# Three buffers instead of two and of four, a later mean square, and weight rounding at priority, in a two-layer hybrid trunk step

## The chip, the cores and the metric

The kernel runs on one core of a Trainium2 chip. The metric is the device time of one execution in microseconds (us). The median of three runs is quoted; one further execution was profiled.

## The reference, cut to what matters

One inference step of two layers over 1024 latent tokens and 256 context tokens, model width 1024. Each layer does:

```
h = rms_norm(x) * (1 + scale) + shift                      # scale, shift, gate from the condition
aq, ak, av, ag, bq, bk, bv, bg, cx, cg, ga, gb, gc = split(h @ w_in)
qa, ka = rope_2d(rms_norm(aq)), rope_2d(rms_norm(ak))      # latents only are rotated
ya = window_attention(qa, ka, av, cached keys, sink) * silu(ag)
qb, kb = rms_norm(bq), rms_norm(bk)                        # per head of 64, over the head's channels
yb = neighbourhood_attention(qb, kb, bv, cached keys, bias) * silu(bg)
yc = rglru(depthwise_conv(cx)) * silu(cg)
z = sigmoid(ga) * (ya @ w_br[0]) + sigmoid(gb) * (yb @ w_br[1]) + sigmoid(gc) * (yc @ w_br[2])
x = x + gate * (z @ w_out)
```

Branch A has 8 query heads and 2 key heads and rotary positions; branch B has 8 heads of each and no rotation. Context tokens read only context tokens. The outputs are the two token arrays and the new keys, values and recurrent states.

## The kernel before, in words

Activations lie with channels on the 128 partitions and tokens along the free dimension, in chunks of 512, 512 (latents) and 256 (context). To hold float32 accuracy, each operand of a projection is split in two parts, hi (rounded) and lo (the rest), and a product takes three matmuls: hi x hi, lo x hi, hi x lo. A weight tile of 128 x 512 is loaded (`load_w`, L415, ring "wr" of 2), rounded on ScalarE to hi (`split_w`, L423) and subtracted on GpSimd to lo (L424), into rings of 4. `job` is one projection of 128 output columns over its chunks: 24 matmuls for each chunk, then an `evac` that takes the result out of PSUM. The weights of the next job are asked for when a job starts.

A planner (class `Weave`) orders TensorE's instructions by hand while the program is written: it adds up an estimated time `now`, runs the attention chain when its parts are due, fills the rest with dense jobs from two queues (`need`: the projections that attention needs; `spare`: gates), and calls functions put off with `W.later(delay, fn)` when `now` reaches them. Delays stand in the table `T`, in ns; `T["ms"]` is the delay of the mean square. TensorE keeps exactly this order. The order on the other engines and on the DMA queue of SyncE is chosen by a scheduler from each instruction's priority, which is its place in the program; `tc.high_priority(AHEAD)` with `AHEAD = 400` gives instructions the priority of a place 400 earlier. Each engine then runs its list in order.

In `attention`, `qk_norm` takes a chunk of q or k out of PSUM: the square on ScalarE (L738, ring "qsq" of 3) and a scaled copy on VectorE (L739, ring "qraw"), both at high priority. `finish`, T["ms"] later, sums the squares over the channels on TensorE (`q_ms`, `k_ms`), makes the reciprocal root on ScalarE and VectorE (L745 to L756) and, in branch A for latents, loads the rotary tables (`cs`, L759, ring "stage") and rotates on GpSimd (L761 to L763). `to_dram` makes the hi and lo parts on GpSimd (L773, L774, ring "stage") and sends them to memory (L780 for k, L869 and L872 for q). For v, `evac` copies to a "qraw" tile (L834), and T["v"] later four transposes and a split on ScalarE (L428) and VectorE (L429) make the parts `vs` in the ring "stage". Cached keys (`kc`) and values (`vc`) are loaded into "qraw" tiles as well. The attention chain works through groups of 256 queries: score products `sc` and `sl` into the PSUM ring "s" of 2, row minima on VectorE (L985, L1001, and L1004 with the sink), exponentials on ScalarE (L1007, L1009), transposes of P (`pt`), their split (`PT`, L428 and L429), and the value products `o`.

Of the kernel before, what the change touches and what calls it, by code (L numbers as in the profile page):

```python
# [9 lines left out]
F32 = mybir.dt.float32  # L10
F32R = mybir.dt.float32r
# [4 lines left out]
P = 128  # L16
# [9 lines left out]
HD = 64  # L26
# [48 lines left out]
AHEAD = 400  # L75
# [1 line left out]
PSB = {"d": 2, "s": 2, "t": 3, "o": 1}  # L77
LGB = ("s", "t")
LDB = ("d", "t")
T = dict(f1=9, f2=2, kc=10000, c0=10000, cq=1, gx=3, nx=8000, yo=1500, yi=1000, aq=9000, ac=7000, ms=2000, v=3200, tok=8600, scale=1100, t0=3400, tb=2200, o=2200, soft=7600, pace=9000, lg=320, lr=8500, cv=16000, le=4200)  # L80


class Weave:
# [107 lines left out]
def trunk(nc, tc, ctx, I, K, O):  # L191
# [22 lines left out]
    def f32(ap):  # L214
        return ap.bitcast(F32)
# [160 lines left out]
    def ada_chain(chunks, ap):  # L376
# [7 lines left out]
        ws = load(quads[0])  # L384
        at = W.now + T["aq"]
        for i, (l, n, h) in enumerate(quads):
# [33 lines left out]
    def split_w(r, name, wp=wp):  # L420
        hi = wp.tile([P, 4, P], F32R, tag="wh", name=f"{name}_h", bufs=4)
        lo = wp.tile([P, 4, P], F32R, tag="wl", name=f"{name}_l", bufs=4)
        nc.scalar.copy(hi, r)  # L423
        nc.gpsimd.tensor_sub(lo, r, f32(hi))  # L424
        return [(hi[:, k], lo[:, k]) for k in range(4)]

    def split(hi, lo, x):
# [300 lines left out]
    def attention(l, H, ap):  # L728
# [2 lines left out]


        def qk_norm(ps, N, gain, rope_c0, name, then, blocks=False):
            raw = ap.tile([P, 512], F32, tag="qraw", name=f"{name}_raw", bufs=4)
            sq = ap.tile([P, 512], F32, tag="qsq", name=f"{name}_sq", bufs=3)
            src, to = (blocked(ps), in_blocks) if blocks else (ps, lambda t: t)
            with tc.high_priority(AHEAD):
                nc.scalar.activation(to(sq[:, :N]), src, AF.Square)  # L738
                nc.vector.tensor_scalar(to(raw[:, :N]), src, gain, None, ALU.mult)  # L739

            def finish():
                ms = ps_tile("t", f"{name}_ms")
                mm(ms[:, :N], blk, sq[:, :N], True, True)
                me = cp.tile([P, 512], F32, tag="g2", name=f"{name}_me", bufs=3)
                nc.vector.tensor_scalar(me[:, :N], ms[:, :N], EPS, None, ALU.add)  # L745
                if not loaded:
                    exp_ln(me[:, :N])
                    loaded.append(True)
                rs = sq

                nc.scalar.activation(rs[:, :N], me[:, :N], AF.Ln)
                nc.scalar.activation(rs[:, :N], rs[:, :N], AF.Exp, scale=-0.5)
                nc.vector.tensor_tensor(raw[:, :N], raw[:, :N], rs[:, :N], ALU.mult)
                nc.scalar.activation(rs[:, :N], rs[:, :N], AF.Square)
                nc.vector.tensor_tensor(rs[:, :N], me[:, :N], rs[:, :N], ALU.mult)
                nc.vector.scalar_tensor_tensor(raw[:, :N], rs[:, :N], -3.0, raw[:, :N], ALU.add, ALU.mult)  # L756
                if rope_c0 is not None:
                    cs = ap.tile([P, 2, 512], F32, tag="stage", name=f"{name}_cs", bufs=2)
                    dma(cs, K["k_rope"][:, :, rope_c0:rope_c0 + N])  # L759
                    nc.vector.stream_shuffle(rs, raw, [(i + 16) % 32 for i in range(32)])  # L760
                    nc.gpsimd.tensor_tensor(rs, rs, cs[:, 1], ALU.mult)  # L761
                    nc.gpsimd.tensor_tensor(raw, raw, cs[:, 0], ALU.mult)
                    nc.gpsimd.tensor_add(raw, raw, rs)  # L763
                then(raw[:, :N])
            W.later(T["ms"], finish)

        def to_dram(x, N, name, put, psum=False):
            st = ap.tile([P, 2, 512], F32R, tag="stage", name=f"{name}_st", bufs=2)
            hi, lo = st[:, 0, :N], st[:, 1, :N]
            if psum:  # L770
                split(hi, lo, x)
            else:
                nc.gpsimd.tensor_copy(hi, x)  # L773
                nc.gpsimd.tensor_sub(lo, x, f32(hi))  # L774
            for h in range(2):
                put(h, f32(st[h * HD:(h + 1) * HD, :, :N]))
# [6 lines left out]
        def k_jobs(br, p, cond):  # L783
            name = f"{br}{l}_{p}"
            perm, rope = br == 1, br == 0
            c0w = O_BK + p * P if br else O_AK
            h0 = 2 * p if br else 0
            out = O[4] if br else O[2]

            def start():  # L790
                t = ap.tile([P, 4, P], F32, tag="qraw", name=f"kc{name}", bufs=4)
                src = I["cache_kb"] if br else I["cache_ka"]
                dma(t, src[0, l, :, h0:h0 + 2].rearrange("(j p) h d -> p j (h d)", p=P))

                def cached():
                    pt = ps_tile("t", f"kct{name}")
                    for j in range(4):
                        transpose(pt[:, j * P:(j + 1) * P], t[:, j], ident)
                    to_dram(pt, NPAST, f"kc{name}", k_put(br, p, NTOK, NPAST), True)
                W.later(T["kc"], cached)  # L800

            def evac(ci, ps):
                c0, N = CHUNKS[ci]

                def then(kn):
                    if c0 >= NLAT:
                        def to_tokens():
                            pt = ps_tile("t", f"kt{name}")
                            for j in range(2):
                                transpose(pt[:, j * P:(j + 1) * P], kn[:, j * P:(j + 1) * P], ident)  # L810
                            ko = ap.tile([P, 2, P], F32, tag="Y", name=f"ko{name}", bufs=2)
                            with tc.high_priority(AHEAD):
                                nc.scalar.copy(ko, pt[:, :2 * P].rearrange("p (j m) -> p j m", j=2))  # L813
                            dma(out[0, l, :, h0:h0 + 2].rearrange("(j p) h d -> p j (h d)", p=P), ko)
                        W.later(T["tok"], to_tokens)
                    to_dram(kn, N, f"k{name}_{ci}", k_put(br, p, c0, N))
                    W.mark(("K", br, l, p, ci), 4000)
                qk_norm(ps, N, dcol[l][:, 2 * br + 1:2 * br + 2], c0 if rope and c0 < NLAT else None,
                        f"k{name}_{ci}", then, perm and c0 < NLAT)
            W.need.append((cond, job(w_in, c0w, (0, 1, 2), lambda ci: H.cols(ci), evac, f"k{name}", start)))  # L820

        def v_jobs(br, p, cond):
            name = f"{br}{l}_{p}"
# [4 lines left out]

            def evac(ci, ps):
                c0, N = CHUNKS[ci]  # L830
                vr = ap.tile([P, 512], F32, tag="qraw", name=f"vr{name}_{ci}", bufs=4)
                lat = perm and c0 < NLAT
                with tc.high_priority(AHEAD):
                    nc.scalar.copy(in_blocks(vr) if lat else vr[:, :N], blocked(ps) if lat else ps)  # L834

                def finish():
                    pt = ps_tile("t", f"vt{name}_{ci}")
                    nb = N // P
                    for j in range(nb):
                        transpose(pt[:, j * P:(j + 1) * P], vr[:, j * P:(j + 1) * P], ident)  # L840
                    src = pt[:, :N].rearrange("p (j h d) -> p j h d", j=nb, h=2)
                    st = ap.tile([P, 4, 2, 2, HD], F32R, tag="stage", name=f"vs{name}_{ci}", bufs=2)
                    split(st[:, :nb, :, 0], st[:, :nb, :, 1], src)
                    if lat:

                        for h in range(2):
                            dma(v_d[l][br][p][ci * HD:(ci + 1) * HD, h:8:2], f32(st[h * HD:(h + 1) * HD]))
                    else:
                        dma(v_d[l][br][p][:, c0 // P:c0 // P + nb], f32(st[:, :nb]))
                    if c0 >= NLAT:  # L850
                        vo = ap.tile([P, 2, P], F32, tag="Y", name=f"vo{name}", bufs=2)
                        nc.scalar.copy(vo, pt[:, :2 * P].rearrange("p (j m) -> p j m", j=2))
                        dma(out[0, l, :, h0:h0 + 2].rearrange("(j p) h d -> p j (h d)", p=P), vo)
                    W.mark(("V", br, l, p, ci), 4000)
                W.later(T["v"], finish)
# [25 lines left out]
        class Keys:  # L881
# [16 lines left out]

            def load_v(c):
                h0 = 2 * c.p if c.br else 0  # L900
                t = ap.tile([P, 4, 2, HD], F32, tag="qraw", name=f"vc{c.name}", bufs=4)
                src = I["cache_vb"] if c.br else I["cache_va"]
                dma(t, src[0, l, :, h0:h0 + 2].rearrange("(j p) h d -> p j h d", p=P))
                c.V = {}
# [653 lines left out]
```

## Time and profile before

| what | us |
|---|---|
| median of 3 runs (3121.65 to 3123.55) | 3122.75 |
| the profiled execution | 3122.02 |
| its span, from the first to the last instruction | 3120.2 |
| TensorE busy in it | 3067.6 |
| VectorE, ScalarE, GpSimd busy | 1781.0, 1707.6, 973.2 |
| mean granted clock of TensorE, of full speed | 0.995 |

Busy time counts an instruction from its start to its end; a bracket at the end of a row of the timeline is the idle time of that engine just before, and what released it. A row of a window has its bounds and length, the busy time of TensorE, of its weight loads, of VectorE, ScalarE and GpSimd with the instructions of each, the granted clock, the DMA share and GB/s. PE is TensorE, PEld its weight loads, DVE VectorE, ACT ScalarE, POOL GpSimd, SPq the queue of SyncE. A clock of 1.00 is 2.4 GHz, 0.50 is 1.2 GHz; a figure between them is a stretch that has both.

### The profile page before, as it was taken

How to read it: one execution, taken by the hardware profiler on the slowest of the kernel's cores; microseconds unless marked ns; L12 is line 12 of the kernel's file. 1: busy time of each engine (PE TensorE's matmuls, PEld its weight loads, DVE VectorE, ACT ScalarE, POOL GpSimd, SP SyncE). 2: the span in 40 equal slices, each digit the busy share in tenths (PEclk: the TensorE clock that was granted, in tenths of full speed). 3: DMA queues.
4: the chain of work that ended last, by engine and by line, in shares of the span. 5: the costliest groups of instructions: out<-in, count | busy, mean ns of one | idle time of the engine just before them, and what ended most of it. 6: DMA issues, size and time to landing. Idle time of an engine off the chain costs nothing. (4 is left out here: it accounts for less than half of the span.)

```text
span 3120.2 us, 48035 instructions
## 1 busy us (share of the span) xinstructions
PE 3067.6 (98%) x17421; PEld 2620.8 (84%) x17421; DVE 1781.0 (57%) x3293; ACT 1707.6 (55%) x3587; POOL 973.2 (31%) x811
## 2 busy tenths in 40 slices
PE   8999999999999999999999999999999999999999
PEld 5777888888888888888878888888888888888887
DVE  5666366666566564356373563665666666655541
ACT  5667365555555664444346873655655656654422
POOL 3454322222222021236243443212232221212632
PEclk9999999999999999999999999999999999999999
DMA  8554545545533332663442226455455332337543
GB/s 290 166 174 133 170 133 159 162 110 163 163 102 86 94 97 77 227 200 127 146 140 68 80 87 181 121 154 147 118 158 153 103 100 78 96 133 238 176 152 102
DMA packets 445322, 433.98 MB, mean 139 GB/s; under 512 B 75056, under 2 KB 366492, under 8 KB 443804
## 3 DMA queue, kind: packets, MB, share of 16 engines
q1 hardware_dynamic: 439100, 413.87, 44.3%
q0 software_dynamic: 5664, 16.83, 1.6%
q8 instruction: 137, 2.24, 0.3%
q14 instruction: 101, 0.83, 0.1%
q10 hardware_dynamic: 320, 0.21, 0.0%
HBM read 297.07 MB, written 137.29 MB: 139 GB/s over the span
## 5 line engine op out<-in xcount | busy, mean ns | idle before, releaser
L428 ACT CAST PT<-pt 128x512 fp32r<-128x512 f32 (+2 forms) x528 | 273.6, 536 | 302.2 <-PE pt L225 298.3
L429 DVE TENSOR_TENSOR PT<-pt,PT 128x512 fp32r<-128x512 f32 (+2 forms) x528 | 321.2, 622 | 102.3 <-ACT PT L428 99.7
L985 DVE TENSOR_REDUCE st<-sc 128x1 f32<-128x512 f32 x256 | 176.1, 688 | 258.4 <-PE sc L218 258.0
L218 PE MATMUL gt<-hhl,wgt_h 128*128 128x512 f32 x736 | 299.0, 406 | 1.3 <-ACT wgt_h L423 1.3
L218 PE MATMUL gt<-hhl,wgt_l 128*128 128x512 f32 x736 | 290.0, 394 | 1.1 <-POOL wgt_l L424 1.1
L218 PE MATMUL gt<-hll,wgt_h 128*128 128x512 f32 x736 | 290.2, 394 | 0.0
L225 PE MATMUL pt<-cst,P 128*128 128x128 f32 x1856 | 272.7, 273 | 0.7 <-ACT ko L813 0.2
L424 POOL TENSOR_TENSOR wgt_l<-wgt_r,wgt_h 128x512 fp32r<-128x512 f32 x110 | 175.2, 1602 | 304.3 <-ACT wgt_h L423 297.3
L225 PEld LDWEIGHTS pt<-cst,P 128*128 128x128 f32 x1856 | 217.6, 141 | 5.8 <-DVE k_me L745 1.4
L218 PE MATMUL po<-z,wpo_h 128*128 128x512 f32 (+1 forms) x768 | 207.5, 358 | 1.2 <-ACT wpo_h L423 1.2
L1007 ACT ACTIVATE P<-sc,st 128x512 f32<-128x512 f32 x256 | 175.1, 684 | 57.7 <-DVE st L1001 55.8
L218 PE MATMUL br<-yl,wbr_h 128*128 128x512 f32 (+1 forms) x576 | 205.2, 356 | 0.6 <-DVE yl L429 0.6
L218 PE MATMUL br<-yh,wbr_h 128*128 128x512 f32 (+1 forms) x576 | 204.7, 355 | 0.0
L218 PE MATMUL br<-yh,wbr_l 128*128 128x512 f32 (+1 forms) x576 | 204.4, 355 | 0.0
L424 POOL TENSOR_TENSOR wsg_l<-wsg_r,wsg_h 128x512 fp32r<-128x512 f32 x48 | 64.6, 1350 | 369.9 <-ACT wsg_h L423 341.6
L1009 ACT ACTIVATE P<-sl,st 128x384 f32<-128x384 f32 (+1 forms) x320 | 170.6, 533 | 13.0 <-DVE st L997 12.8
L218 PE MATMUL o<-PT,Vpast 128*128 128x256 f32 x1024 | 176.0, 293 | 0.9 <-DVE PT L429 0.3
L218 PE MATMUL sc<-Kpast,Q 128*128 128x512 f32 x512 | 168.9, 411 | 7.2 <-ACT P L1007 7.1
L218 PEld LDWEIGHTS gt<-hhl,wgt_l 128*128 128x128 f32 x736 | 138.6, 188 | 33.8 <-POOL wgt_l L424 1.5
L218 PEld LDWEIGHTS gt<-hhl,wgt_h 128*128 128x128 f32 x736 | 138.8, 189 | 32.3 <-issue 4.7
L218 PEld LDWEIGHTS gt<-hll,wgt_h 128*128 128x128 f32 x736 | 139.1, 189 | 25.7 <-issue 0.5
L218 PE MATMUL sg<-hhl,wsg_h 128*128 128x512 f32 x384 | 155.7, 405 | 0.0
(350 smaller groups left out, 8495.5 us busy)
## 6 DMA issues: line engine op xcount, KB each, us to landing
Q<-q_d SPq DMA_DIRECT2D x160, 256.0 KB
gl<-g_d SPq DMA_DIRECT2D x48, 640.0 KB
wgt_r<-in_w_in_dram SPq DMA_DIRECT2D x110, 256.0 KB
g_d<-tgt SPq DMA_DIRECT2D x92, 256.0 KB
wa<-in_w_ada_dram POOLq DMA_DIRECT2D x64, 256.0 KB, 4.1
yg<-y_d SPq DMA_DIRECT2D x24, 640.0 KB
yr<-s_d SPq DMA_DIRECT2D x24, 640.0 KB
wpo_r<-in_w_out_dram SPq DMA_DIRECT2D x60, 256.0 KB
```

The costliest lines, as they stand in the source:

```text
L218: nc.tensor.matmul(out, a, b, start=start, stop=stop)
L225: nc.tensor.transpose(out, x, idn)
L424: nc.gpsimd.tensor_sub(lo, r, f32(hi))
L428: nc.scalar.copy(hi, x)
L429: nc.vector.tensor_sub(lo, x, f32(hi))
L985: nc.vector.tensor_reduce(cm, psc, AX.X, ALU.min)
L1007: nc.scalar.activation(pt[:, nl * P:(nl + 4) * P], psc, AF.Exp, bias=m, scale=-1.0, accum_out=sums[:, t, x, 1:2])
L1009: nc.scalar.activation(pt[:, :nl * P], loc, AF.Exp, bias=m, scale=-1.0, accum_out=sums[:, t, x, 0:1])
```

## The change

The ring "stage" gets three buffers instead of two, for the parts and for the rotary tables. The ring "qraw" gets three instead of four, for raw q, k and v and for the cached keys and values. The mean square is planned 3.2 us instead of 2.0 us after the eviction. The rounding of weights and its subtraction get high priority, in every stage of the kernel. The number of instructions does not change.

```diff
-T = dict(... ms=2000, v=3200, ...)
+T = dict(... ms=3200, v=3200, ...)
...
     def split_w(r, name, wp=wp):
         hi = wp.tile([P, 4, P], F32R, tag="wh", name=f"{name}_h", bufs=4)
         lo = wp.tile([P, 4, P], F32R, tag="wl", name=f"{name}_l", bufs=4)
-        nc.scalar.copy(hi, r)
-        nc.gpsimd.tensor_sub(lo, r, f32(hi))
+        with tc.high_priority(AHEAD):
+            nc.scalar.copy(hi, r)
+            nc.gpsimd.tensor_sub(lo, r, f32(hi))
...
         def qk_norm(ps, N, gain, rope_c0, name, then, blocks=False):
-            raw = ap.tile([P, 512], F32, tag="qraw", name=f"{name}_raw", bufs=4)
+            raw = ap.tile([P, 512], F32, tag="qraw", name=f"{name}_raw", bufs=3)
...
-                    cs = ap.tile([P, 2, 512], F32, tag="stage", name=f"{name}_cs", bufs=2)
+                    cs = ap.tile([P, 2, 512], F32, tag="stage", name=f"{name}_cs", bufs=3)
...
         def to_dram(x, N, name, put, psum=False):
-            st = ap.tile([P, 2, 512], F32R, tag="stage", name=f"{name}_st", bufs=2)
+            st = ap.tile([P, 2, 512], F32R, tag="stage", name=f"{name}_st", bufs=3)
...
-                vr = ap.tile([P, 512], F32, tag="qraw", name=f"vr{name}_{ci}", bufs=4)
+                vr = ap.tile([P, 512], F32, tag="qraw", name=f"vr{name}_{ci}", bufs=3)
...
-                    st = ap.tile([P, 4, 2, 2, HD], F32R, tag="stage", name=f"vs{name}_{ci}", bufs=2)
+                    st = ap.tile([P, 4, 2, 2, HD], F32R, tag="stage", name=f"vs{name}_{ci}", bufs=3)
```

The "qraw" tiles of the cached keys and values change from 4 to 3 buffers in the same way.

## Rows read from the trace of the kernel before

**Rows 1.** The page, part 1: engine, busy us, share of span, instructions

```profile
PE 3067.6 (98%) x17421; PEld 2620.8 (84%) x17421; DVE 1781.0 (57%) x3293; ACT 1707.6 (55%) x3587; POOL 973.2 (31%) x811
```

**Rows 2.** TensorE waits, whole span: releaser, us in total, times, longest

```profile
PE sc L218 <- ACT P L1007: 7.1, 15, 0.9
PE q_ms L218 <- ACT q_sq L738: 4.9, 2, 2.5
```

**Rows 3.** Timeline, layer 0, 801 to 808 us: start, length, instruction, [wait before]

```profile
801.61 2.92 SPq L872 DMA_DIRECT2D q_d<-q_st  x4
...
805.97 0.59 ACT L428 CAST vs<-vt 128x512 fp32r<-128x512 f32 x1 [6.98 <-DMA q_d<-q_st]
...
807.09 0.39 PE L218 MATMUL o<-PT,Vlat 128*128 128x256 f32 x1 [3.86 <-ACT PT L428]
807.93 1.92 PE L218 MATMUL o<-PT,Vlat 128*128 128x256 f32 x7 [0.45 <-DVE PT L429]
```

**Rows 4.** Windows of 5 us, layer 0: busy by engine, granted clock, DMA

```profile
805.00:810.00 5.00, 2.46 (x9) 1.94 (x10) 1.71 (x3) 2.96 (x8) 0.00 (x0) 0.84 0.60 209
810.00:815.00 5.00, 5.00 (x22) 4.71 (x22) 2.76 (x5) 2.39 (x6) 0.00 (x0) 0.50 0.00 0
```

**Rows 5.** Timeline, layer 1, 2358 to 2363 us, ScalarE and TensorE

```profile
2358.20 0.59 ACT L428 CAST vs<-vt 128x512 fp32r<-128x512 f32 x1 [2.44 <-DMA q_d<-q_st]
...
2361.40 0.62 PE L218 MATMUL o<-PT,Vlat 128*128 128x256 f32 x3 [1.26 <-DVE PT L429]
2362.39 1.01 PE L218 MATMUL o<-PT,Vlat 128*128 128x128 f32 x4 [0.37 <-ACT PT L428]
```

**Rows 6.** Timeline, first q of branch A, layer 0: evictions, last read

```profile
768.13 0.61 ACT L738 ACTIVATE q_sq<-q 128x512 f32<-128x512 f32 x1
...
784.75 0.39 ACT L738 ACTIVATE q_sq<-q 128x256 f32<-128x256 f32 x1
...
786.25 1.83 POOL L774 TENSOR_TENSOR q_st<-q_raw,q_st 128x512 fp32r<-128x512 f32 x1
```

**Rows 7.** Timeline and one window, mean squares: 891 to 900 us, 2447 us

```profile
891.71 2.98 POOL L424 TENSOR_TENSOR wgt_l<-wgt_r,wgt_h 128x512 fp32r<-128x512 f32 x2
...
893.47 1.23 DVE L1004 TENSOR_TENSOR st<-st,sink 128x1 f32<-128x1 f32 x1
...
895.51 0.19 ACT L1007 ACTIVATION_READ_ACCUMULATOR P<-sc,st 128x1 f32 x1
...
896.59 0.75 PE L218 MATMUL q_ms<-q_sq,cst 128*128 128x256 f32 x2 [2.52 <-ACT q_sq L738]
...
895.00:900.00 5.00, 3.42 (x12) 3.07 (x13) 3.79 (x11) 2.05 (x7) 0.00 (x0) 0.71 0.55 161
...
2447.85 0.70 PE L218 MATMUL q_ms<-q_sq,cst 128*128 128x256 f32 x2 [2.42 <-ACT q_sq L738]
```

**Rows 8.** Timeline and one window, weights: 233 to 265 us, 1592 to 1595 us

```profile
233.14 3.03 SPq L415 DMA_DIRECT2D wgt_r<-in_w_in_dram  x2
...
258.73 1.15 ACT L423 CAST wgt_h<-wgt_r 128x512 fp32r<-128x512 f32 x2
...
259.41 0.50 PE L218 MATMUL gt<-hhl,wgt_h 128*128 128x512 f32 x1 [1.28 <-ACT wgt_h L423]
...
261.25 0.50 PE L218 MATMUL gt<-hhl,wgt_l 128*128 128x512 f32 x1 [1.10 <-POOL wgt_l L424]
...
260.00:265.00 5.00, 3.90 (x12) 2.97 (x12) 5.00 (x4) 1.04 (x1) 3.62 (x3) 0.72 0.20 59
...
1592.63 0.73 PE L218 MATMUL po<-z,wpo_h 128*128 128x512 f32 x2 [1.17 <-ACT wpo_h L423]
1594.21 0.50 PE L218 MATMUL po<-z,wpo_l 128*128 128x512 f32 x1 [0.84 <-POOL wpo_l L424]
```

**Rows 9.** ScalarE's waits, whole span: weight roundings that wait for loads

```profile
ACT wgt_h L423 <- DMA wgt_r<-in_w_in_dram: 28.1, 16, 5.1
...
ACT wk_h L423 <- DMA wk_r<-in_w_in_dram: 5.7, 5, 2.5
```

More of the change, by code (lines that the diff above doesn't have):

```diff
@@ L79 @@
 LDB = ("d", "t")
-T = dict(f1=9, f2=2, kc=10000, c0=10000, cq=1, gx=3, nx=8000, yo=1500, yi=1000, aq=9000, ac=7000, ms=2000, v=3200, tok=8600, scale=1100, t0=3400, tb=2200, o=2200, soft=7600, pace=9000, lg=320, lr=8500, cv=16000, le=4200)
+T = dict(f1=9, f2=2, kc=10000, c0=10000, cq=1, gx=3, nx=8000, yo=1500, yi=1000, aq=9000, ac=7000, ms=3200, v=3200, tok=8600, scale=1100, t0=3400, tb=2200, o=2200, soft=7600, pace=9000, lg=320, lr=8500, cv=16000, le=4200)
 class Weave:
@@ L790, in start @@
             def start():
-                t = ap.tile([P, 4, P], F32, tag="qraw", name=f"kc{name}", bufs=4)
+                t = ap.tile([P, 4, P], F32, tag="qraw", name=f"kc{name}", bufs=3)
                 src = I["cache_kb"] if br else I["cache_ka"]
@@ L900, in load_v @@
                 h0 = 2 * c.p if c.br else 0
-                t = ap.tile([P, 4, 2, HD], F32, tag="qraw", name=f"vc{c.name}", bufs=4)
+                t = ap.tile([P, 4, 2, HD], F32, tag="qraw", name=f"vc{c.name}", bufs=3)
                 src = I["cache_vb"] if c.br else I["cache_va"]
```

## The prediction

> **What bounds the kernel now.** I read the page's busy shares first. TensorE is busy 98% of the span and the other engines are far below it [rows 1], so adding or removing work on ScalarE, VectorE or GpSimd matters only where TensorE waits for it, and the change adds and removes none: it moves work and resizes rings. What it can win is TensorE's idle time, 3120.2 - 3067.6 = 52.6 us, and what the engine loses while its clock is granted at the lower of its two levels (1.2 instead of 2.4 GHz). The second view is TensorE's list of waits, then the timeline of TensorE window by window, because the sizes of single waits tell which part of the change could touch them. In the attention stages the waits are few and long, except for a row of short ones, the score product waiting for an exponential that frees its PSUM bank, 15 waits of 7.1 us in total [rows 2]. The third view is the windows of 5 us, for the clock behind each long wait.
>
> **Part 1: a third buffer for the parts ("stage", 2 to 3).** The ring holds both the hi/lo parts on their way to memory and the rotary tables. In layer 0 the parts of two q chunks fill both slots. Their four transfers are issued from 801.61 us on; the parts of v, which come next on ScalarE, wait 6.98 us for such a transfer to land [rows 3]. ScalarE runs in order, so the rounding of P transposes queued behind it comes late too, and TensorE waits 3.86 us and then 0.45 us more for those: 4.31 us [rows 3]. From there its clock is at the lower level: granted 0.84 in 805 to 810 and 0.50 in 810 to 815 us [rows 4], with TensorE busy nearly all the time after the wait. The loss is 0.16 x 5 + 0.50 x 5 = 3.3 us. With a third slot the v parts go ahead when ScalarE comes to them, at 805.97 - 6.98 = 799.0 us. Next would be the P parts: about 0.6 us of ScalarE for v, 0.6 for P and 0.7 of VectorE, done by about 802 us if nothing else comes first, ahead of the product that began at 807.09 after 3.86 us of wait, so wanted at 803.2. So both go, 4.3 + 3.3 = 7.6 us. In layer 1 the same v parts wait 2.44 us and TensorE 1.26 + 0.37 = 1.6 us [rows 5], with no loss of clock. Sum of part 1: 9.2 us. The lower bound is 1.6 us, if in layer 0 a new wait of the same kind takes the old one's place.
>
> **Part 2: the ring of raw q, k, v (4 to 3).** A slot is held from the eviction to the last read by GpSimd. The densest stretch is the first q of branch A: chunks evicted at 768.13 and 784.75 us (one more between them) are all alive when the first one's parts finish at 786.25 + 1.83 = 788.1 us [rows 6]. Walking through all evictions and last reads of layer 0 in this way I find three alive at most, never four. The squares beside them have had three buffers all along. I take 0. Were a slot late, its wait would sit at the head of ScalarE or VectorE as in part 1, up to 7.6 us.
>
> **Part 3: mean squares planned 3.2 instead of 2.0 us after the eviction.** This moves each mean-square product some 1.2 us of planned TensorE work later in TensorE's fixed order. Only two of them wait, once in each layer, 2.52 and 2.42 us [rows 7]. In the first, the square that it needs stands on ScalarE behind two exponentials; the scores that follow in TensorE's order need the bank that the first of these frees at about 895.70 us [rows 7]. So when the mean square steps back, the score becomes the next to wait, until 895.7 instead of 896.6: 0.9 us saved, 1.8 in both layers. The clock behind the first wait (granted 0.71 in 895 to 900 us, 0.29 x 5 = 1.5 us [rows 7]) I leave lost. Bounds: all of it, 2.52 + 2.42 + 1.5 = 6.4 us, and a loss of 2 x 1.2 = 2.4 us if in each layer the first group of attention starts that much later (its keys and queries are marked ready later) and nothing fills its end.
>
> **Part 4: rounding of weights at priority.** The ScalarE rounding and the GpSimd subtraction move ahead of what up to 400 program places before them had. TensorE waits for weights at two places. At 259 us the two loads were issued in one stretch from 233.14 us to 236.2, and ScalarE rounds them only at 258.73; the waits are 1.28 and 1.10 us, and the clock in 260 to 265 us is 0.72, that is 1.4 us lost [rows 8]. In the output projection the waits are 1.17 and 0.84 us [rows 8]. All four go if the rounding steps in front of the work that held ScalarE: 1.28 + 1.10 + 1.4 + 1.17 + 0.84 = 5.8 us. I take 5.3, since at 1592 us the subtraction of 1.5 us on GpSimd still follows a load that came late. Lower bound 0: the rounding is there but the engine was not free.
>
> **What it costs.** Each rounding put in front takes 1.15 / 2 = 0.58 us of ScalarE [rows 8]. If each of the 15 score waits met one, that is 15 x 0.58 = 8.7 us; if none, 0. I take a figure nearer the low end, 2.5 us, because the longest of these waits is 0.9 us [rows 2], so most exponentials have room ahead of them. GpSimd's subtractions in new places: 1.0 us (the price of one is in the first rival). The later marks of part 3: 0.5 us of the 2.4.
>
> Sum: 9.2 + 0 + 1.8 + 5.3 = 16.3 us won, 4.0 lost, 12.3 us net. The profiled execution took 3122.0 us, so 3109.7; the median of the runs stands 0.7 us above it, so 3110 us, 0.4% less.
>
> **The rivals.** First, **new places for GpSimd's subtractions eat the gain**. Just before the stall of 896 us GpSimd does two weight subtractions back to back, 891.71 to 894.69; VectorE's update of one column of the row minimum takes 1.23 us and ends at 894.70, with GpSimd [rows 7]. The exponentials wait for it, and TensorE behind them: 2.52 us and 1.5 us of clock, 4.0 us for one such meeting. The Trainium skill (SBUF — State Buffer, Who interferes with whom) has the rule for it: a VectorE instruction with two SBUF inputs and a GpSimd one that reads SBUF exclude each other for the whole instruction. The trace agrees in the 1.23 us. By that rule the priority that I count as a gain also steers such subtractions, and part 4 would be no gain at all. Worked out from rows: the meetings now number two. Three more cost 12 us and leave nothing of the 12.3: 3122 us. Against it: GpSimd is not given more work, and VectorE's rows there mostly run past it. A similar end is reached if layer 0's long wait for a slot merely moves (7.6 us) and one meeting is new.
>
> Second, on the other side, **roundings come to the head of ScalarE before their load has landed**. It happens now 16 times for the gate weights, 28.1 us in total and 5.1 at most, and 5 times for k's weights, 2.5 at most [rows 9]; almost all in stages where ScalarE has slack. Priority can place a rounding there in the attention stages too, where ScalarE's queue holds the exponentials. There a hold of 2.44 us cost TensorE 1.6, one of 6.98 cost 4.31 and the clock [rows 3 to 5]. The gain of 12.3 is gone after eight holds of 2.44 us (8 x 1.6 = 12.8); by twelve the kernel is 7 us slower. I price it at sixteen: 25.6 - 12.3 = 13 us slower, 3136 us. Against it: a rounding was already older in program order than most of its neighbours, so priority shifts it by a few instructions.
>
> Third, **the priority changes nothing** because the roundings were already first when they were ready. Then part 4's 5.3 us are missing, with the 3.5 us of cost that go with them: 3112 us, still faster. It lies inside the forecast's range.
>
> **How the numbers follow.** A difference of 0.2%, 6.2 us, is about what a measurement of this kernel can tell from no change. Forecast with the third rival: 0.61, range 3100 to 3117. First rival: 0.23, 3115 to 3131. Second: 0.16, from 3124 up. Faster than 3116.5: 0.58 of the 0.61 and 0.03 of the first rival, 0.61. Slower than 3129: 0.03 of the first and 0.13 of the second, 0.16. The rest, 0.23, is within. The low end is 9.2 + 6.4 + 5.8 = 21.4 us won at no cost, 3101, less a little for score waits that go along: 3100. The high end takes in the first rival, 3128; above it are 0.16, below 3100 some 0.04.
>
> **What would show it.** In the profile after: no rounding of v's parts that waits for a transfer of q's parts, no TensorE wait above 3 us behind it near 805 us, and the granted clock at 1.00 there. The mean-square waits of 2.4 to 2.5 us down to at most 1.6, as a score waiting for an exponential instead. No wait for wgt or wpo in TensorE's list. The score waits still about 7 to 10 us in total. Span about 3107 to 3108 us, TensorE idle about 45 us. Wrong would be: a new wait of several us for a raw slot at ScalarE's or VectorE's head; roundings waiting for their load among the exponentials; or one-column VectorE updates of more than 1 us at new places.

## The result, and the profile after

The changed kernel takes 3160.5 us (median of four runs) beside 3122.2 for the kernel before: ratio 1.012 [1.0108, 1.0133], 38 us slower. The prediction was 3110, 3100 to 3128. The profiled execution has a span of 3157.6 us at a mean granted clock of 0.991; before it was 3120.2 at 0.995. From L423 on, line numbers are one higher: the rounding of weights is L424, ScalarE's split L429, the exponentials L1008, the keys' loads L897, the stores of q's parts L873.

The page, part 1, as in [rows 1]:

```profile
PE 3079.1 (98%) x17421; PEld 2629.1 (83%) x17421; DVE 1767.2 (56%) x3293; ACT 1708.0 (54%) x3589; POOL 955.5 (30%) x811
```

TensorE's idle time is 3157.6 - 3079.1 = 78.5 us, 25.9 more than before; the other 11.5 us of the span are busy time, from the same 17421 matmuls at a lower clock or in another order. TensorE's waits over the whole span, as in [rows 2] (releaser, us in total, times, longest):

```profile
PE sc L218 <- ACT P L1008: 17.6, 14, 3.0
PE sl L218 <- DMA Klat<-k_d: 13.6, 4, 4.7
PE sc L218 <- DMA Kpast<-k_d: 7.6, 1, 7.6
```

Two things stand out. Scores wait for the keys' loads, 21.2 us in five waits; before there were two such waits, of 0.8 us together. And scores wait for exponentials up to 3.0 us at a time, where 0.9 was the longest. The worst reload, in layer 0, on the queue of SyncE and on TensorE (start, length, instruction, [wait before]):

```profile
840.45 0.49 PE L218 MATMUL sl<-Klat,Q 128*128 128x256 f32 x2
...
844.03 0.54 SPq L415 DMA_DIRECT2D wq_r<-in_w_in_dram  x1
852.05 2.91 SPq L873 DMA_DIRECT2D q_d<-q_st  x4
855.06 0.56 SPq L897 DMA_DIRECT2D Kpast<-k_d  x1
855.71 0.56 SPq L897 DMA_DIRECT2D Klat<-k_d  x1
...
860.57 1.22 PE L218 MATMUL sc<-Kpast,Q 128*128 128x512 f32 x2 [7.62 <-DMA Kpast<-k_d]
864.75 0.80 PE L218 MATMUL sl<-Klat,Q 128*128 128x256 f32 x2 [2.96 <-DMA Klat<-k_d]
```

The last score on the old keys is at 840.45, so the keys' one buffer is free soon after. But their loads are issued only at 855.06, because four stores of q's parts stand in front of them on SyncE's queue, and those wait for GpSimd to make the parts. SyncE's own waits in 844 to 853 us:

```profile
SPq L873 <- POOL q_st L774: 7.7, 1, 7.7
```

GpSimd in turn had stood for the rotary table of these q (`q_cs`), a load issued on the same queue at 840.02 us:

```profile
846.07 1.29 POOL L762 TENSOR_TENSOR q_sq<-q_sq,q_cs 128x512 f32<-128x512 f32 x1 [6.25 <-DMA q_cs<-k_rope]
...
851.97 0.40 POOL L774 CAST q_st<-q_raw 128x256 fp32r<-128x256 f32 x1
```

The same reload in the kernel before: the loads leave 0.7 us after the start of the last score on the old keys and are there in time.

```profile
817.27 0.41 PE L218 MATMUL sl<-Klat,Q 128*128 128x256 f32 x2
...
817.95 0.58 SPq L896 DMA_DIRECT2D Kpast<-k_d  x1
...
829.83 0.62 PE L218 MATMUL sc<-Kpast,Q 128*128 128x512 f32 x2
```

The second loss shows at the end of attention in layer 1. Windows of the last 40 us of that attention, with the gate jobs `sg` alone (busy time of TensorE, its weight loads and ScalarE, granted clock, DMA), the kernel before:

```profile
2744.30:2764.30 20.00, 13.03 (x63) 10.04 (x63) 1.56 (x3) 1.00 0.21 66
2764.30:2784.30 20.00, 8.37 (x42) 6.47 (x43) 0.98 (x2) 1.00 0.17 54
```

and the changed one, first the same view, then all instructions:

```profile
2781.10:2801.10 20.00, 0.83 (x8) 0.63 (x6) 0.38 (x1) 0.83 0.13 40
2801.10:2821.10 20.00, 0.06 (x1) 0.08 (x1) 0.00 (x0) 1.00 0.02 7
...
2781.10:2801.10 20.00, 12.67 (x64) 9.80 (x63) 11.06 (x27) 11.52 (x34) 2.49 (x2) 0.83 0.13 40
2801.10:2821.10 20.00, 13.80 (x93) 11.05 (x91) 11.06 (x25) 9.08 (x23) 0.00 (x0) 1.00 0.02 7
```

Before, 21.4 us of gate work stood between the chain's steps there. After, there is 0.9 us, and TensorE is busy 26.5 of 40 us: it waits for each exponential in turn.

```profile
2786.14 0.73 PE L218 MATMUL sc<-Kpast,Q 128*128 128x512 f32 x2 [2.96 <-ACT P L1008]
2790.44 1.22 PE L218 MATMUL sc<-Kpast,Q 128*128 128x512 f32 x2 [1.99 <-ACT P L1008]
2795.60 0.73 PE L218 MATMUL sc<-Kpast,Q 128*128 128x512 f32 x2 [1.59 <-ACT P L1008]
```

The gate work was used up earlier. Counting `gt` and `sg` matmuls in TensorE's timeline of layer 1 between the first scores of one set of keys and the next gives 132, 90, 126, 90 and then, up to the last value product, 897 for the last set before, and 144, 144, 144, 111 and 792 after: 105 fewer are left for the end. The first four sets take 447.6 us before and 461.9 after, so 14.3 of the 21.4 us that layer 1's attention loses are lost there, while the additional gate matmuls run; at the end the chain doesn't make them up.

### The profile page after: what moved, and what is told of

It is laid out like the page before. It is cut to its first block, busy times and chain, and to the rows that moved or that the text cites. A ratio compares the mean times of both kernels' runs of the same rounds, so it can differ in the third digit from the quotient of the medians.

```text
span 3157.6 us, 48074 instructions
## 1 busy us (share of the span) xinstructions
PE 3079.1 (98%) x17421; PEld 2629.1 (83%) x17421; DVE 1767.2 (56%) x3293; ACT 1708.0 (54%) x3589; POOL 955.5 (30%) x811
## 4 chain that ended last, share of the span: by engine, by line
PE 83%; DVE 5%; ACT 4%; DMA 4%; POOL 2%; issue 2%; SPq 0%; ACTq 0%; DVEq 0%; POOLq 0%
PE gt L218 19%; PE sg L218 10%; PE br L218 7%; PE o L218 7%; PE pt L225 6%; PE po L218 6%; PE q L218 6%; PE k L218 4%; PE v L218 4%; PE sc L218 4%; PE sl L218 3%; PE cx L218 2%; PE lg L218 1%; DMA Klat<-k_d 1%; PE q_ms L218 1%
## 5 line engine op out<-in xcount | busy, mean ns | idle before, releaser
L429 ACT CAST PT<-pt 128x512 fp32r<-128x512 f32 (+2 forms) x528 | 274.0, 535 | 378.7 <-PE pt L225 374.4
L425 POOL TENSOR_TENSOR wgt_l<-wgt_r,wgt_h 128x512 fp32r<-128x512 f32 x110 | 153.3, 1402 | 352.7 <-ACT wgt_h L424 331.8
L1008 ACT ACTIVATE P<-sc,st 128x512 f32<-128x512 f32 x256 | 175.3, 685 | 49.8 <-DVE st L1002 48.6
```

What stands on the lines that cost most here:

```text
L429: nc.scalar.copy(hi, x)
L1008: nc.scalar.activation(pt[:, nl * P:(nl + 4) * P], psc, AF.Exp, bias=m, scale=-1.0, accum_out=sums[:, t, x, 1:2])
```

## The experiments

Each is the kernel before with the edit shown, unless said otherwise. Three points split a span: layer 1's first score, layer 1's first branch product (`br`, the stage after attention) and the end. In the second part three gate jobs that are held back (216 matmuls) stand between the last value product of attention and `br`, save in the two kernels with the tail filled. In us of the profiled execution, with the ratio to the kernel before and its interval:

| kernel | ratio | to first score, layer 1 | from there to `br` | rest |
|---|---|---|---|---|
| before | 1 | 1933.4 | 893.0 | 293.8 |
| after | 1.012 [1.0108, 1.0133] | 1948.7 | 914.4 | 294.5 |
| rings_alone | 0.9974 [0.9963, 0.9986] | 1928.6 | 891.3 | 294.4 |
| prio_alone | 1.0006 [0.9995, 1.0017] | 1940.2 | 892.7 | 298.2 |
| rings_prio | 0.9983 [0.9974, 0.9993] | 1927.9 | 892.5 | 298.1 |
| ms_alone | 1.0103 [1.0084, 1.0123] | 1946.5 | 910.7 | 294.6 |
| ms2600 | 1.0052 [1.0037, 1.0067] | 1945.3 | 896.9 | 293.9 |
| ms2800 | 1.0078 [1.0063, 1.0093] | 1937.7 | 913.6 | 297.0 |
| ms3200_k_on_act | 1.0053 [1.0036, 1.0069] | 1929.3 | 916.7 | 294.6 |
| ms2600_k_on_act | 1.0035 [1.0022, 1.0049] | 1934.9 | 901.8 | 294.2 |
| ms3200_layer1_only | 1.0067 [1.0052, 1.0082] | 1931.0 | 915.0 | 293.9 |
| ms3200_tail_filled | 1.0112 [1.0097, 1.0127] | 1945.7 | 898.1 | 311.7 |
| ms3200_tail_k_on_act | 1.0063 [1.0046, 1.0080] | 1932.8 | 896.1 | 312.7 |
| ms3200_early_start | 0.9990 [0.9981, 1.0000] | 1933.8 | 888.9 | 298.2 |
| after_early_start | 0.9999 [0.9990, 1.0008] | 1936.3 | 889.3 | 297.0 |
| rings_early_start | 1.0018 [1.0009, 1.0027] | 1935.7 | 894.2 | 294.2 |
| rings_early_k_on_act | 1.0037 [1.0024, 1.0049] | 1944.9 | 897.0 | 294.1 |

A profiled execution can lie some us off its median (prio_alone by 7), so single columns are read to a few us.

**The parts of the change, one by one.**

```diff
-ms=2000
+ms=3200
```

> The kernel before with one edit: the mean square planned 3.2 instead of 2.0 us after the eviction. Theory M (the delay reorders TensorE's fixed list, so that the reloads of K at a change of keys and the end of attention come too late for it): 3150 to 3165 us, with waits for Klat or Kpast of 2.5 to 8 us each as in the changed kernel. Theory P (rounding at priority): 3117 to 3127 us. Theory R (the rings): 3117 to 3127 us.

3156.4 us, 33.7 above before. The later mean square alone is nearly the whole loss, with the same two kinds of wait, 16.9 us for the keys and 18.4 us for exponentials:

```profile
PE sc L218 <- ACT P L1007: 18.4, 12, 3.0
PE sl L218 <- DMA Klat<-k_d: 10.8, 4, 3.3
PE sc L218 <- DMA Kpast<-k_d: 6.1, 1, 6.1
```

```diff
-tag="stage", ... bufs=2   (3 places)      -tag="qraw", ... bufs=4   (4 places)
+tag="stage", ... bufs=3                   +tag="qraw", ... bufs=3
```

> The kernel before with the two rings of the change (three for parts, three for raw q, k, v) and nothing else. TensorE's order is that of before. Theory R (a load of cached keys or values that waits for a raw slot holds the SyncE queue): 3145 to 3165 us. Theories M and P: 3112 to 3118 us, since the wait of 6.98 us of v's parts near 806 us and the 4.31 us of TensorE behind it are gone, with the 3.3 us of clock; in layer 1 another 1.6 us.

3115.9 us, 6.8 less than before. TensorE's order is that of the kernel before, and the stall of [rows 3] is gone: v's parts on ScalarE, the product behind them, and the window of [rows 4].

```profile
802.50 0.58 ACT L428 CAST vs<-vt 128x512 fp32r<-128x512 f32 x1
...
806.68 1.03 PE L218 MATMUL o<-PT,Vlat 128*128 128x256 f32 x8
...
805.00:810.00 5.00, 5.00 (x35) 4.54 (x34) 2.65 (x8) 2.97 (x8) 0.00 (x0) 1.00 0.42 149
```

```diff
+        with tc.high_priority(AHEAD):
             nc.scalar.copy(hi, r)
             nc.gpsimd.tensor_sub(lo, r, f32(hi))
```

> The kernel before with one edit: rounding and subtraction of weights at priority. Theory P (the roundings and subtractions get in front of the exponentials and of the parts whose stores stand ahead of the K loads on the SyncE queue): 3145 to 3165 us. Theory M: 3115 to 3125 us, within 0.2% of before. Theory R: the same as M.

> The changed kernel with the mean square planned 2.0 us after the eviction again, so rings and priority without the delay. Theory M: 3108 to 3120 us, and no wait of TensorE for Klat or Kpast above 1 us. Theory P: 3145 to 3165 us. Theory R: 3145 to 3165 us.

The priority alone gives 3125.6 us, no change that can be measured. On top of the rings it gives 3119.7, 3.8 more than the rings alone, with intervals that overlap. The waits for weights in prio_alone (to compare with [rows 8]):

```profile
262.88 0.50 PE L218 MATMUL gt<-hhl,wgt_h 128*128 128x512 f32 x1 [1.28 <-ACT wgt_h L424]
264.70 0.67 PE L218 MATMUL gt<-hhl,wgt_l 128*128 128x512 f32 x1 [1.09 <-POOL wgt_l L425]
1600.56 0.50 PE L218 MATMUL po<-z,wpo_l 128*128 128x512 f32 x1 [0.86 <-POOL wpo_l L425]
```

Of the four, only the 1.17 us at 1592 is gone. On ScalarE the rounding of the first two still follows the copies of `tgt`, as it does in the kernel before. The kernel before, then prio_alone:

```profile
258.00 0.84 ACT L711 COPY tgt<-gt 128x512 f32<-128x512 f32 x2
...
261.47 0.84 ACT L712 COPY tgt<-gt 128x512 f32<-128x512 f32 x2
262.19 1.15 ACT L424 CAST wgt_h<-wgt_r 128x512 fp32r<-128x512 f32 x2
```

**How the loss grows with the delay.** The same edit with 2600 and with 2800.

> The kernel before with the mean square planned 2.6 us after the eviction. In the trace of the delay of 3.2 us alone a whole gate job of 72 matmuls stands between the first scores on new keys and the projection of the keys after those, where before the projection came first. Theory S (a step: the delay moves the mark that frees that projection past the boundary of a dense job, which then cannot be broken off; by the planner's own time that happens between 2.6 and 2.8 us): 3117 to 3127 us, no wait for Klat or Kpast above 1 us. Theory L (each 0.2 us of delay costs its share of the 34 us): 3136 to 3144 us.

> The kernel before with the mean square planned 2.8 us after the eviction, just past the step of theory S. Theory S: 3150 to 3160 us, nearly the whole 34 us, with waits for Klat or Kpast of 2.5 to 6 us each. Theory L: 3141 to 3149 us.

3139.3 and 3147.3 us. In total time there is no step, and the expectation of one failed. The table shows two terms. Layer 1's attention does step, 897 us at 2.6 and 914 at 2.8 (893 before), as the expectation had it. The part up to layer 1's first score does not grow in step with the delay: 11.9, 4.3 and 13.1 us at 2.6, 2.8 and 3.2, each from one profile. At 2.6 us most of the loss is there, and TensorE waits for the keys again:

```profile
499.02 0.79 PE L218 MATMUL sl<-Klat,Q 128*128 128x256 f32 x2 [4.76 <-DMA Klat<-k_d]
612.54 0.51 PE L218 MATMUL sl<-Klat,Q 128*128 128x256 f32 x2 [1.20 <-DMA Klat<-k_d]
729.95 0.51 PE L218 MATMUL sl<-Klat,Q 128*128 128x256 f32 x2 [2.58 <-DMA Klat<-k_d]
```

**The keys' loads taken off SyncE's queue.**

```diff
-                    dma(f32(c.K[n]), src[:, :, c0:c0 + N])
+                    nc.scalar.dma_start(f32(c.K[n]), src[:, :, c0:c0 + N])
```

> The delay of 3.2 us alone, with the loads of K issued from ScalarE's queue instead of SyncE's, so that no store of v's or q's parts that waits for its data stands in front of them. Theory Q (the waits for K, 17 us, come from the order of SyncE's queue; the end of attention in layer 1 is a loss of its own): K waits gone, the waits at the end of layer 1's attention stay, 3131 to 3141 us. Theory K (K is late because it was made late): the K waits stay, 3150 to 3160 us.

> The kernel before with ms = 2600 and the loads of the keys (Kpast, Klat) issued from ScalarE's queue instead of SyncE's. At 2600 with SyncE's queue the time was 3139.3 us, 16 above before, and TensorE waited for the keys' loads 4.76, 1.20 and 2.58 us. Theory Q (those 16 us are mainly the reload of the keys behind SyncE's stores): the 8.5 us of waits and what follows them go, 3123 to 3133 us. Rival E (the 16 us are the chain itself that ends later, whatever queue loads the keys): 3136 to 3142 us.

At 3.2 us the time is 3139.9, 16.5 less than ms_alone. All that is left of the waits for keys is 0.6 us, and layer 1's first score comes 17.2 us sooner, which is even 4.1 us sooner than in the kernel before. What the other queue does without the delay was not run, so part of the 17.2 may be a gain of its own. Layer 1's attention is as long as in the changed kernel:

```profile
PE sc L218 <- ACT P L1007: 21.7, 14, 3.0
...
PE sl L218 <- DMA Klat<-k_d: 0.6, 2, 0.4
```

At 2.6 us it gives 3133.8, just outside either range. The waits for keys are gone, and 5.5 us of the 16 come back; layer 1's first score is 10.4 us sooner and 4.9 of it are lost in layer 1. So the queue is about a third of the loss at 2.6. The waits of values for VectorE's `Y` are as large with either queue, 8.7 and 8.5 us where they were 0.7 before; what they cost was not tested.

**The keys' projections let go earlier.** The mark `start` of a group lets the next set's projections begin. Here it is set one score step earlier, with ms = 3200.

```diff
-                if g.t0 == 0:
+                if i == 0:
                     W.mark(("start", g.br, l, g.p))
...
                     behind.append((g, s))
+                    if s == 0 and nxt and nxt.t0 == 0:
+                        W.mark(("start", nxt.br, l, nxt.p))
```

> The delay of 3.2 us alone, with the mark that frees the next keys' projections set one score step (about 12 us of plan) earlier. Theory S: the projections no longer stand behind a gate job, attention ends earlier in the plan than before, 3108 to 3124 us, with the delay kept. Theory L: 3145 to 3160 us.

> The changed kernel whole, with that mark set one score step earlier. Theory S: nearly all of the 38 us go. With ms = 3200 alone the earlier mark gave 3121.5 us; the rings took off 6.8 us by themselves and the priority put some 4 on: 3114 to 3123 us. Rival (the rings and the priority have a loss of their own with ms = 3200): 3130 us and above.

3121.5 us with the delay alone and 3121.6 with the changed kernel whole: the 34 and the 38 us are gone with the delay in place. Waits for the keys are not all gone, 2.7 us in the first and 6.0 in the second. In layer 1 the gate matmuls between sets of keys are now, with the delay alone, 144, 87, 84, 87 and 933, and the first four sets take 441.4 us: 402 gate matmuls in them, 438 before and 543 in the changed kernel go with 441.4, 447.6 and 461.9 us. In the last 20 us of its attention, `sg` alone:

```profile
2760.50:2780.50 20.00, 12.32 (x60) 8.81 (x58) 1.18 (x2) 1.00 0.10 35
```

> The kernel before with the rings of the change alone (stage 3, qraw 3), ms = 2000, and the mark that frees the next keys' projections set one score step earlier. The rings alone took 3115.9 us. Theory S (a projection that misses a boundary of dense jobs is what costs, and an earlier mark leaves room): the plan's attention ends 4 to 5 us earlier, of which some comes through, 3108 to 3116 us. Rival C (projections that come earlier bring their stores in front of the reload of the keys on SyncE's queue, as in the kernel after): 3118 to 3130 us.

> The second kernel of this call with the keys' loads on ScalarE's queue as well. Theory Q (what is left of TensorE's waits for the keys comes from SyncE's queue): 2 to 8 us less than that kernel. Rival (with the early mark no load of the keys stands behind a store that waits, and the issue on ScalarE only delays exponentials): the same or up to 6 us more.

With the rings and the old delay the earlier mark doesn't help: 3126.7 us, 11 more than the rings alone. The number is in the range of the rival, but not by its mechanism, for the waits for keys come to 0.4 us. What is new is values and transposes that wait for VectorE:

```profile
PE o L218 <- DVE Y L1070: 7.5, 4, 2.3
...
PE rt L225 <- DVE k_me L745: 3.1, 2, 1.6
PE pt L225 <- DVE k_me L745: 2.8, 2, 1.5
```

With the keys on ScalarE's queue as well it is 3132.6, 6 more. Here, where the waits for keys were 0.4 us, the other queue had nothing to save, and the time is longer.

**One loss or two.** Delay of 3.2 us in layer 1 alone; then, with 3.2 us in both, two of the three gate jobs that layer 1 holds back for the next stage given to its attention, without and with the keys on ScalarE's queue.

```diff
-            W.later(T["ms"], finish)
+            W.later(3200 if l else T["ms"], finish)
```

```diff
+            back = 1 if l else 3
-            W.spare.extend((always, j()) for j in jobs[:-3])
+            W.spare.extend((always, j()) for j in jobs[:-back])
```

> The kernel before with the mean square planned 3.2 us after the eviction in layer 1 alone; layer 0 keeps 2.0. Read from stage boundaries, the delay in both layers costs about 13 us up to layer 1's first score and about 18 us from there to the end of layer 1's attention. Theory of two separate terms: only the second is left, 3137 to 3145 us, and the first score of layer 1 stands where it stood before (1933 us). Rival (one loss that builds up over both layers, half in each or more in the second only because the first is late): outside that, below 3134 or above 3148 us.

> The kernel before with ms = 3200, and of layer 1's three gate jobs that are held back for the stage after attention two are given to attention as dense work (one is held back). Theory T (in layer 1 the dense work is used up some 40 us before the end of attention, so the chain waits bare there): the idle of TensorE in the last 40 us of that attention, about 12 us, and the clock behind it, 3 us, mostly go: 3139 to 3149 us against 3156 with three held back. Rival (the chain itself ends later, dense work or not; the two jobs are then missing as cover in the next stage): 3152 to 3162 us.

> Both cures at ms = 3200: the keys loaded from ScalarE's queue and two more gate jobs in layer 1's attention. With the first alone 3139.9 us. If the two terms add up and these are all, 3122 to 3130 us. If they are one loss seen twice, 3135 us and above.

In layer 1 alone the delay costs 20.8 us (3144.0), and layer 1's first score stands where it did (1931.0 and 1933.4): layer 1's term does not need layer 0's. With the tail filled the time is 3156.8, as without. TensorE has no wait in the 60 us before it comes to `br`, and `br` comes 12.6 us sooner after the first score than in ms_alone. But that is because two of the jobs in front of it have moved; the attention itself ends later. Its last value products, in ms_alone and with the tail filled:

```profile
2814.48 0.62 PE L218 MATMUL o<-PT,Vlat 128*128 128x256 f32 x3 [0.34 <-DVE PT L429]
...
2824.39 0.63 PE L218 MATMUL o<-PT,Vlat 128*128 128x256 f32 x4
```

From layer 1's first score that is 868.0 and 878.7 us. The rest is 17 us longer, for the stage whose cover was taken away waits for attention's results:

```profile
2843.80 0.50 PE L218 MATMUL br<-yh,wbr_h 128*128 128x512 f32 x1 [3.87 <-ACT yh L428]
...
2861.03 0.80 PE L218 MATMUL br<-yh,wbr_h 128*128 128x512 f32 x1 [4.99 <-ACT yh L428]
...
2855.00:2860.00 5.00, 1.04 (x2) 0.32 (x2) 1.17 (x1) 2.06 (x3) 0.00 (x0) 0.50 0.96 326
```

So the expectation that filling the tail saves its idle time was right for the idle time and wrong for the kernel. Its rival describes the run: the chain ends late, dense work or not, and the two jobs are then missing as cover. With both edits, 3142.9: the queue's gain again (14 us), the tail's none. That lies in the range given for one loss seen twice, but layer 1 alone has shown the two apart; it is the cure of the tail that fails.

## Why the prediction was wrong

**Part 3 failed**, by its lower bound. For the mean squares themselves it was right, and small: the 2.52 and 2.42 us of [rows 7] became 0.80 each.

```profile
909.50 1.13 PE L218 MATMUL q_ms<-q_sq,cst 128*128 128x512 f32 x2 [0.80 <-DVE PT L430]
```

That is 3.3 us won where 1.8 were forecast. The step that failed is "a loss of 2 x 1.2 = 2.4 us if in each layer the first group of attention starts that much later". It counted the later marks once in each layer and in time alone, and left out that every set of keys and queries passes through them, and that TensorE's order, written from planned times, changes with them. Measured alone, part 3 costs 33.7 us:
- Up to layer 1's first score it costs 13.1 us. The projections' parts come out later against the chain, so their stores stand on SyncE's queue ahead of the keys' reload and hold it. The other queue takes 17.2 us off this column, and the waits for keys with it.
- In layer 1 it costs 17.7 us. More gate matmuls go between the first sets of keys, and the chain runs late there; 105 fewer are left for the last set, and the chain is bare for its last 40 us. The earlier mark puts the gate work back and takes 21.8 us off this column. Gate work lent by the next stage fills the bare end and wins nothing, so the idle time at the end is the sign of the late chain, not the loss itself.

That the gate jobs go first because the mark comes after a boundary between two jobs, and a job isn't broken off, is what the planner's code suggests; the runs show the counts and the cure, not that boundary itself.

**Part 1 was right in its mechanism**, and about right in size: 6.8 us by itself, with an interval of 4 to 12, where 9.2 were forecast. In the changed kernel there seems to be nothing of it to be had, since the later mean square moves that meeting by itself. In ms_alone v's parts wait longer for the transfer than before, and no value product waits for it, for the chain stands for the keys:

```profile
852.42 0.59 ACT L428 CAST vs<-vt 128x512 fp32r<-128x512 f32 x1 [8.82 <-DMA q_d<-q_st]
```

**Part 2** was nothing with the old delay, as forecast: in rings_alone no eviction waits for a raw slot. In the changed kernel one does for 2.84 us, which the forecast named as a sign of being wrong; TensorE stands for the keys from 852.95 us on, so it isn't what holds it. Two of 1.47 us on VectorE in layer 1 stand in ms_alone too, with four slots.

```profile
852.06 0.59 ACT L835 COPY vr<-v 128x512 f32<-128x512 f32 x1 [2.84 <-POOL q_st L775]
```

**Part 4 was wrong**: 5.3 us were forecast, and of the waits 1.17 us went. The forecast had the rounding at 259 us step in front of the work that held ScalarE. It did not: with priority it runs behind the same copies, and the two waits keep their length to 0.01 us. Why the scheduler left it there stays open. The third rival, that the priority changes nothing, describes it.

The sum of the parts run alone, -6.8 + 2.8 + 33.7 = 29.7 us, is 8.6 short of the 38.3: without the gain of part 1 it is 36.5. That the delay makes this gain void is argued, for no run joins the rings and the delay without the priority. The interval of ms_alone by itself is 26 to 38 us, so the 8.6 could also be noise.

**The rivals.** GpSimd's subtractions did not eat anything: updates of one column of the row minimum (L1004 before, L1005 after) that take over 1 us number six before, six with the priority alone and two after. The forecast had counted two before, those with a long wait of TensorE behind them. Roundings of gate weights that wait for their loads on ScalarE rose from 28.1 us in 16 waits to 33.3 in 16; none of these waits lies within an attention stage, where the second rival had placed them. The forecast had a slower kernel at 0.16, by the second rival; it came by none of the three.

ScalarE's queue for the keys is a point where a rule and a run differ. The Trainium skill (DMA: Bandwidth & Descriptors, Issuing engines are not separate DMA queues) says that issuing from several engines saves only the time of the issue, usually small. Here it saved 16.5 us with the delay, because the issuing engine also waits, in order, for the data of what stands in front, 7.7 us in the changed kernel's worst reload, where an issue itself took 0.56 us. With the rings and the earlier mark the same edit cost 6 us.

## What to carry to other kernels

Where one engine's order is written from planned times, a delay in the plan is a change of the whole order: price it by what the marks behind it release, in every round of the loop, not by the instruction that moves. Before moving a store, look at what is queued behind it on its issuing engine, above all reloads into a single buffer. And work that fills gaps is a stock: what goes early holds the chain and is missing at the end, and what is borrowed from the next stage is paid there. Last, try the parts of a change alone. Here the rings by themselves are the best kernel measured, 0.9974 of the time before.

## What the runs showed of the hardware

The clock falls behind long waits as in [rows 4], and for longer behind the reload. Windows of the changed kernel:

```profile
855.00:860.00 5.00, 0.00 (x0) 0.00 (x0) 0.00 (x0) 0.00 (x0) 0.00 (x0) 0.54 0.90 264
860.00:865.00 5.00, 1.47 (x3) 0.76 (x4) 0.69 (x1) 0.00 (x0) 0.00 (x0) 0.50 0.97 312
865.00:870.00 5.00, 5.00 (x23) 4.72 (x24) 2.69 (x6) 2.97 (x9) 0.00 (x0) 0.59 0.51 178
```

All four compute engines stand for 5 us while the DMA engines are busy 90%, and the clock is still at 0.59 in the window after them, in which TensorE is busy throughout: 0.46 x 5 + 0.50 x 5 + 0.41 x 5 = 6.9 us of full speed are not granted, of which only the last 2.1 fall on matmuls back to back. The Klat load issued at 855.71, behind q's stores and the Kpast load, lets TensorE go at 864.75, 9.0 us later.
